# Opening and gate stage of a hybrid backbone step: instruction order written out by hand, row copies on ScalarE, half of the transposes moved behind the modulation

## The chip, the cores and the metric

The kernel runs on one core of a Trainium2 chip. The metric is the device time of one execution in microseconds (us). A change of more than 0.2% (4.4 us) either way counts here as faster or slower.

## The reference, cut to what matters

One layer of a backbone is computed for two groups of tokens, 2048 sample tokens and 128 prompt tokens, each with D = 1024 channels. The part that the change touches is the beginning:

```python
def ada_mod(cvec, w, b):
    m = jnp.einsum('...d,de->...e', jax.nn.silu(cvec), w) + b
    return jnp.split(m, 3, axis=-1)
...
    shift, scale, gate = ada_mod(c, w_ada[l], b_ada[l])
    xn = rmsnorm(h, ln_g[l]) * (1.0 + scale[:, None, :]) + shift[:, None, :]
    # in mixer:
    proj = jnp.einsum('btd,de->bte', xn, w_in)
    # z_a: 512 columns of proj; silu(z_a) gates branch A
```

Everything behind it (the rest of the projection, a delta-rule scan, a spatial gating branch, a Fourier branch, the merge and the output projection) is unchanged.

## The kernel before

**Numbers.** Each f32 operand of a matmul is split into a high and a low f16 part, and three products are summed: high by high, high by low and low by high. `xh` and `xl` hold the two parts of the modulated, normalised input, turned so that channels lie on partitions (8 blocks `k` of 128 channels by 2176 tokens). A weight block is handled by the generator `converting` (from L262): ScalarE squares it and sums, VectorE casts the sum (L234), TensorE sums over the partitions, VectorE makes a power-of-two scale (L243 to L245), ScalarE writes the high part (L290), VectorE the low part (L291). `zlo` and `zhi` are these parts for the four blocks of `z_a`.

**Opening.** The shift and the scale come from 16 blocks of `w_ada`, each 512 KB, loaded into a ring of 7 buffers (`ab`). Six of them (6, 7, 12 to 15) are stored turned: VectorE multiplies such a block with a row of SiLU(cond) and sums (`column_sums`, L490, one instruction for each of the two groups). The other ten go in pairs through TensorE (`block_pair`): eight f32 matmuls give two rows of 256 sums, VectorE copies them out of PSUM (`adr`, L497), and TensorE turns them into columns in the bank `pa` (L499). Between these blocks the first 512 token rows (`x0`, four loads) arrive. TensorE turns them, 8 blocks of 4 transposes (L543), and ScalarE copies each block out (L544). ScalarE also squares the rows (L460), which gives a factor per token. `row_scale` spreads it over partitions by matmuls and copies it to `rsb` (L473). `bound(0)` adds the bias to the shift and `bound(1)` makes the scale, with a bound from which a common power of two `sx` follows; then both are multiplied with it. The loads stand in one list:

```python
LOADS = ("a0", "a1", "d6", "x0", "x1", "x2", "a2", "a3", "x3", "d7", "a4", "a5", "w0", "d12", "a8", "a9", "w1", "d13", "d14", "a10", "d15", "a11")
```

Here `a` is a block for TensorE, `d` one for VectorE, `x` a quarter of the rows, and `w` a weight block of `z_a`. The loads are kept in this order on SyncE's queue. The first two weights are converted inside this stage, the other two in the gate stage.

**Gate stage.** The tokens are taken in five groups `ti`: four of 512 and one of 128 (the prompt). For each group and each `k`, VectorE multiplies `x` with the scale and `rsb` (L612), ScalarE adds the shift and rounds to `xh` (L613), and the low part is the rest. VectorE makes the low part in one instruction (L627), GpSimd in two (L623, L624). GpSimd has `k` = 2 and 5 of the first group and all odd `k` of the others. `silu_za` then runs 24 matmuls of 512 columns for each of four blocks of `z_a`: first blocks 0 and 1 together, then 2, then 3. `finish` takes a block out of PSUM: ScalarE a sigmoid (L601), VectorE the product (L602), SyncE the store. `row_scale` for the next group stands after the first two blocks.

**Order.** The program is traced in the order in which it is written, and a planner then lays out each engine's instruction stream by priority and by simulated readiness. The stream of an engine can thus differ from the order of the text. `tc.issue_after(i)` forces instructions of an engine behind the instruction `i` of the same engine, and costs no wait on another engine. Before, some ten such places hold single instructions back. Waits between engines follow from the data, and each engine works through its stream in order.

Of the kernel before, what the change touches and what calls it, by code (L numbers as in the profile page):

```python
# [11 lines left out]
F16 = mybir.dt.float16  # L12
# [26 lines left out]
LOADS = ("a0", "a1", "d6", "x0", "x1", "x2", "a2", "a3", "x3", "d7", "a4", "a5", "w0", "d12", "a8", "a9", "w1", "d13", "d14", "a10", "d15", "a11")  # L39
# [129 lines left out]

@with_exitstack  # L170
def hybrid_flow_kernel(ctx: ExitStack, tc: tile.TileContext, x_prompt, x_sample, state_delta, c, c_ctx, w_ada,
# [3 lines left out]
    V, A, G, PE, SY = nc.vector, nc.scalar, nc.gpsimd, nc.tensor, nc.sync  # L175
# [237 lines left out]
    warm = sb(cp, [P, 1], "warm")  # L413
    A.activation(warm, mhalf, AF.Sigmoid)
# [36 lines left out]
    def norms(xs, early=False, after=None):  # L451

        xss = sb(p0p, [P, len(xs)], "xss")
        for j, x in enumerate(xs):
            jk = spare(after is not None and j == 3) if early else sb(p0p, [P, D], "xm", F16, bufs=4)
            with tc.issue_after(after[min(j // 2, 1) + j // 3].ins) if after is not None else ExitStack():
                if after is not None and j == 3:
                    V.scalar_tensor_tensor(jk, x, 1.0, x, ALU.mult, ALU.mult, accum_out=xss[:, j:j + 1])
                else:
                    A.activation(jk, x, AF.Square, accum_out=xss[:, j:j + 1])  # L460
        rs = sb(p0p, [P, len(xs)], "rs")
        rsqrt(rs, xss, 1.0 / D, len(xs))
        return rs

    def row_scale(ti, xs, after=None):

        t0, tn = TBS[ti]
        rs = norms(xs, ti < 2, after)
        ps = bank(ps_x, [P, len(xs), P])
        for j in range(len(xs)):  # L470
            mm(ps[:, j, :], rs[:, j:j + 1].to_broadcast([P, P]), ident)
        rsb = sb(p0p, [P, tn], "rsb", bufs=1)
        V.tensor_copy(rsb, ps.rearrange("p j t -> p (j t)"))  # L473
        return rsb

    rowc = [sb(p0p, [P, D], "rowc") for g in range(2)]
    for g in range(2):
        for half in range(2):
            ps = bank(ps_mm, [P, 4, P])
            for k in range(4):  # L480
                mm(ps[:, k, :], scT[:, half * 4 + k, g:g + 1].to_broadcast([P, P]), ident)
            A.copy(rowc[g][:, half * 512:half * 512 + 512], ps.rearrange("p k c -> p (k c)"))
# [3 lines left out]
    raw0 = sb(p0p, [P, KT, 512], "xt")  # L486

    def column_sums(b, st):
        for g in range(2):
            V.scalar_tensor_tensor(spare(1), st, 1.0, rowc[g], ALU.mult, ALU.mult, accum_out=ada[:, b, g:g + 1])  # L490

    def block_pair(b, sts):
        ps = bank(ps_d, [2, 256])
        for k in range(KT):
            mm(ps, scT[:, k, :], sts[k // 4][:, k % 4 * 256:(k % 4 + 1) * 256], k == 0, k == KT - 1)
        adr = sb(p0p, [2, 256], "adr", bufs=1)
        V.tensor_copy(adr, ps)  # L497
        for k in range(2):
            PE.transpose(pa[:, b + k, :], adr[:, k * P:(k + 1) * P], ident[:2, :2])  # L499

# [14 lines left out]
    x0, half = None, None  # L515
    for what in LOADS:
        kind, n_ = what[0], int(what[1:])
        if kind == "w":
            read_next()
            fetch(n_ + 1)  # L520
            while len(wdone) - len(wsteps) <= n_:
                weight_step()
            wlate[0] = 0
            continue
        st = sb(p0p, [P, 4, D], "xt") if what == "x0" else None if kind == "x" else sb(p0p, [P, D], "ab", bufs=7)
        if kind == "x":
            x0 = st if n_ == 0 else x0
            st = x0[:, n_, :]
        load(st, xrows(n_ * P, P) if kind == "x" else w_adb[n_])
        if kind == "d":  # L530
            column_sums(n_, st)
        elif kind == "a" and n_ % 2:
            if n_ == 11:
                bound(0)
            block_pair(n_ - 1, (half, st))
        elif kind == "a":
            half = st
        elif n_ == 3:
            x0 = [x0[:, j, :] for j in range(4)]
            for k in range(KT):  # L540
                ps = bank(ps_mm, [P, 512])
                for j in range(4):
                    PE.transpose(ps[:, j * P:(j + 1) * P], x0[j][:, k * P:(k + 1) * P], ident)  # L543
                A.copy(raw0[:, k, :], ps)  # L544
            rsb = row_scale(0, x0)
# [14 lines left out]
    with tc.high_priority():  # L560
        bound(1)
        bs16 = sb(cp, [P, 1], "bs16", BF16)
        V.tensor_add(bs16, bss[:, 0:1], bss[:, 1:2])
        sx, isx = scales(None, cp, "xsc", bs16)
        V.tensor_scalar(ms, ms, sx, None, ALU.mult)
        V.tensor_scalar(sh, sh, sx, None, ALU.mult)
        for w in wdone:
            V.tensor_mul(w.inv, w.own, isx)
# [5 lines left out]
    def silu_za(ti, gs, between=None):  # L574
# [8 lines left out]
        for i, phase in enumerate(phases):  # L583
            if i == 1 and between is not None:
                between()
# [6 lines left out]
        else:  # L592
            with tc.issue_after(zaw[3].made.ins), tc.issue_after(zaw[3].low.ins):
                finish(ti, gs, pss)
# [1185 lines left out]
```

## Time and profile before

| | |
|---|---|
| time, median of 3 runs | 2192.6 us (2190.14 to 2194.45) |
| profiled execution, its own time | 2190.57 us |
| span of its profile | 2188.8 us |
| TensorE busy | 2110.8 us (96%) |
| VectorE, ScalarE, GpSimd busy | 1314.2, 1034.0, 735.5 us |
| mean granted TensorE clock | 0.988 |

Start times are in us from the span's start. In a row of the timeline stand the start, the duration, the engine and line, the operation, output and input by name, shapes and count; in brackets the idle time before it and what ended that. PE is TensorE, DVE VectorE, ACT ScalarE, POOL GpSimd. A row that merges n matmuls shows a span that is a little longer than n times their pitch, since matmuls overlap. The gate stage's first matmul begins at 43.56 us, and the next stage's first at 151.19 us.

### The profile page before, as it was taken

To read this page: it belongs to the slowest core of one execution; us is meant where nothing else is said; L and a number is where in the kernel's file an instruction comes from. 1 tells how busy PE (TensorE), PEld (TensorE's weight loads), DVE (VectorE), ACT (ScalarE), POOL (GpSimd) and SP (SyncE) were. 2 spreads that over 40 slices of the span, in tenths; PEclk is the share of its full clock that TensorE was granted. 3 is DMA by queue.
4 is the path that set the end of the run, shared out by engine and by line. 5 is a ranking of instruction groups with operands and counts; after the bars stand their busy time and mean duration, and the time that the engine had idled before them with its cause. 6 is when DMAs were issued, how large, how long until landed. Compare 5 with 4: busy or idle time off the path is not lost. (4 is left out here: it accounts for less than half of the span.)

```text
span 2188.8 us, 42552 instructions
## 1 busy us (share of the span) xinstructions
PE 2110.8 (96%) x16249; PEld 1206.4 (55%) x16249; DVE 1314.2 (60%) x3035; ACT 1034.0 (47%) x2372; POOL 735.5 (34%) x889
## 2 busy tenths in 40 slices
PE   7899999999899999999899999899999999999998
PEld 3354444455455577778555555555655444444444
DVE  5646854479878697456665555765564544233454
ACT  4544744466555574445644445655553422222332
POOL 2531332223334332443322223355443222122543
PEclk9999999999999999999999999999999999999999
DMA  8524832177776653434645546766664433323542
GB/s 340 192 95 153 287 118 100 61 221 232 232 230 216 213 170 105 122 115 140 217 163 168 164 160 190 231 200 209 205 199 157 164 125 118 131 101 119 177 149 106
DMA packets 228012, 371.90 MB, mean 170 GB/s; under 512 B 38728, under 2 KB 125152, under 8 KB 225376
## 3 DMA queue, kind: packets, MB, share of 16 engines
q1 hardware_dynamic: 175424, 274.20, 38.6%
q0 software_dynamic: 12688, 51.27, 6.6%
q10 hardware_dynamic: 39696, 43.72, 6.0%
q8 instruction: 127, 2.08, 0.4%
q14 instruction: 77, 0.63, 0.1%
HBM read 241.48 MB, written 127.62 MB: 169 GB/s over the span
## 5 line engine op out<-in xcount | busy, mean ns | idle before, releaser
L220 PE MATMUL b<-xh,whi 128*128 128x512 f16 (+1 forms) x1920 | 651.9, 348 | 7.5 <-DVE sg L1325 5.7
L220 PE MATMUL b<-xl,whi 128*128 128x512 f16 (+1 forms) x1920 | 652.6, 348 | 0.0
L220 PE MATMUL b<-xh,wlo 128*128 128x512 f16 (+1 forms) x1920 | 651.1, 348 | 0.0
L220 PEld LDWEIGHTS <-whi 128*128 128x128 f16 x3904 | 356.5, 98 | 336.7 <-issue 18.5
L220 PEld LDWEIGHTS <-wlo 128*128 128x128 f16 x1952 | 191.5, 98 | 177.6 <-issue 3.8
L220 PE MATMUL b<-big,bhi 128*128 128x512 f16 (+1 forms) x960 | 250.7, 347 | 3.4 <-ACT big L1557 2.5
L1597 POOL TENSOR_TENSOR mrow<-mrow,sg 128x512 f32<-128x512 f32 (+1 forms) x80 | 95.4, 1193 | 284.5 <-DVE sg L1596 175.6
L220 PE MATMUL b<-big,blo 128*128 128x512 f16 (+1 forms) x480 | 162.9, 347 | 0.2 <-DVE blo L291 0.2
L1587 ACT ACTIVATE sg<-b,winv 128x512 f32<-128x512 f32 (+1 forms) x120 | 74.2, 618 | 135.0 <-PE b L220 134.2
L220 PEld LDWEIGHTS <-xh 128*128 128x128 f16 x1496 | 117.0, 98 | 30.3 <-DVE yT L1510 1.9
L1596 DVE SCALAR_TENSOR_TENSOR sg<-b,binv,sg 128x512 f32<-128x512 f32 (+1 forms) x80 | 53.4, 668 | 129.1 <-PE b L220 121.4
L220 PEld LDWEIGHTS <-bhi 128*128 128x128 f16 x960 | 86.4, 98 | 80.2 <-issue 3.6
L827 POOL TENSOR_TENSOR cy<-cy,raw 128x545 f32<-128x545 f32 (+1 forms) x48 | 65.7, 1397 | 186.3 <-ACT raw L826 186.3
L234 DVE CAST wscb<-wss 128x1 bf16<-128x1 f32 x93 | 14.2, 153 | 143.7 <-ACT wlo L278 59.7
L220 PE MATMUL b<-whi,xh 128*128 128x128 f16 x544 | 92.9, 219 | 2.3 <-DVE yT L1510 1.7
L1060 POOL COPY T<-ES 32x256 f16<-32x256 f16 x68 | 27.1, 399 | 198.1 <-DMA ES<-ei 193.2
L220 PE MATMUL b<-whi,xl 128*128 128x128 f16 x544 | 92.9, 219 | 0.0
L220 PE MATMUL b<-wlo,xh 128*128 128x128 f16 x544 | 92.9, 219 | 0.0
L220 PE MATMUL b<-wohi,ml 128*128 128x512 f16 (+2 forms) x248 | 91.7, 372 | 0.5 <-DVE ml L1668 0.5
L220 PE MATMUL b<-wohi,mh 128*128 128x512 f16 (+2 forms) x248 | 91.9, 372 | 0.0
L220 PE MATMUL b<-wolo,mh 128*128 128x512 f16 (+2 forms) x248 | 91.9, 372 | 0.0
L291 DVE SCALAR_TENSOR_TENSOR wlo<-wst,wsc,whi 128x1024 f16<-128x1024 f32 x52 | 69.0, 1327 | 32.6 <-ACT whi L290 32.4
(476 smaller groups left out, 4283.0 us busy)
## 6 DMA issues: line engine op xcount, KB each, us to landing
wst<-in_w_blk_dram SPq DMA_DIRECT2D x58, 512.0 KB, 5.0
qkv<-cy POOLq DMA_DIRECT2D x12, 1089.0 KB, 5.3
st<-br SPq DMA_DIRECT2D x48, 256.0 KB, 3.9
mrow<-mrg SPq DMA_DIRECT2D x18, 512.0 KB, 3.7
mrow<-mrg SPq DMA_DIRECT2D x16, 576.0 KB, 3.9
mrg<-mrow POOLq DMA_DIRECT2D x16, 576.0 KB, 3.7
dc<-dec SPq DMA_DIRECT2D x17, 512.0 KB, 4.7
kq<-qkv SPq DMA_DIRECT2D x34, 256.0 KB, 4.2
```

The lines of the kernel that those rows point to most:

```text
L220: PE.matmul(out, l, r, start=start, stop=stop)
L234: V.tensor_copy(sb16, ss)
L291: w.low = V.scalar_tensor_tensor(w.lo, st, s, w.hi, ALU.mult, ALU.subtract)
L827: G.tensor_tensor(y[:, c0:c1], y[:, c0:c1], raw[:, 1 + c0:1 + c1], ALU.mult)
L1060: G.tensor_copy(T16[rows(a0, b), :, :, b], ES[0:32, :, 2 * a0 + b, :, wT])
L1587: A.activation(sg, ps, AF.Sigmoid, scale=gw.inv)
L1596: V.scalar_tensor_tensor(sg, ps, binv[:, 1:2], sg, ALU.mult, ALU.mult)
L1597: G.tensor_tensor(mr, mr, sg, ALU.add)
```

## The change

Three helpers of the kernel, the handles for VectorE, ScalarE and TensorE, are wrapped. While `kept` is set, each instruction of such an engine is put behind the one written before it on the same engine, so that its stream is the text's order. GpSimd and SyncE are not wrapped. `kept` is set from the opening to the end of the gate stage, but for the conversion of the small weight `w_bd` and for the weight steps of the next stage (`loose_steps`). The text itself is rewritten:

- The loads come as a0 a1 d6, x0 to x3, d7 a2 a3, d12 a4 a5 w0, d13 w1, a8 a9, d14 a10 d15 a11.
- The copies of the pairs' row sums (`row_copy`) and the copy of the first `rsb` go to ScalarE.
- Of the 8 blocks of transposes of `x0`, four stay around the second pair's matmuls, and four come behind the last pair's (`turn_x0`).
- The first multiply of the gate stage comes ahead of the scaling of the shift.
- In the first group VectorE makes all eight low parts. In the others GpSimd makes those of `k` = 5 and 7 only.
- The conversion of the weights 2 and 3 is threaded through the first group. Their scales come in the middle of the products with the low part.
- The factor of the next group's rows is spread after block 2, ahead of block 3, and block 3 is taken out of PSUM behind the fourth multiply of the next group.

```diff
+class _InTurn:
+    def __init__(self, tc, engine):
+        self.tc, self.engine, self.kept, self.last = tc, engine, False, None
+    def __getattr__(self, name):
+        f = getattr(self.engine, name)
+        if not self.kept:
+            return f
+        def call(*args, **kw):
+            with self.tc.issue_after(self.last.ins) if self.last is not None else ExitStack():
+                self.last = f(*args, **kw)
+            return self.last
+        return call
...
-    V, A, G, PE, SY = nc.vector, nc.scalar, nc.gpsimd, nc.tensor, nc.sync
+    G, SY = nc.gpsimd, nc.sync
+    V, A, PE = [_InTurn(tc, e_) for e_ in (nc.vector, nc.scalar, nc.tensor)]
...
+    V.kept = A.kept = PE.kept = True
...
+    def row_copy(ps):
+        adr = sb(p0p, [2, 256], "adr", bufs=1)
+        A.copy(adr, ps)
+        return adr
+    def turn_x0(k):
+        ps = bank(ps_mm, [P, 512])
+        for j in range(4):
+            PE.transpose(ps[:, j * P:(j + 1) * P], x0[:, j, k * P:(k + 1) * P], ident)
+        A.copy(raw0[:, k, :], ps)
...
+    p_ = block_pair(0)
+    column_sums(6, 0)
+    squares(x0s, xss0, (0, 1), True)
+    column_sums(6, 1)
+    adr = row_copy(p_)
+    turn_rows(0, adr)
...
+    rsb = spread(rs, A)
+    column_sums(12, 0)
+    column_sums(12, 1)
+    fetch_blocks(13)
+    read_next()
+    p_ = block_pair(4)
...
+    step0()
+    adr = row_copy(p_)
+    column_sums(13, 0)
+    step0()
+    fetch_blocks(8, 9)
+    turn_rows(4, adr)
+    step0()
+    step1()
+    column_sums(13, 1)
+    step1()
+    step0()
+    fetch_blocks(14, 10, 15, 11)
+    p_ = block_pair(8)
+    step1()
+    step1()
+    adr = row_copy(p_)
+    turn_rows(8, adr)
+    bound(0)
+    column_sums(14, 0)
+    column_sums(14, 1)
+    p_ = block_pair(10)
+    column_sums(15, 0)
+    column_sums(15, 1)
+    adr = row_copy(p_)
+    turn_x0(4)
+    turn_x0(5)
+    turn_rows(10, adr)
+    turn_x0(6)
+    turn_x0(7)
...
+        def low(k):
+            x, hi, lo = part_of(k)
+            if ti and k in (5, 7):
                 G.tensor_scalar(x, x, sh[:, k, g:g + 1], None, ALU.add)
                 G.tensor_tensor(lo, x, hi, ALU.subtract)
             else:
+                V.scalar_tensor_tensor(lo, x, sh[:, k, g:g + 1], hi, ALU.add, ALU.subtract)
+        for k in range(KT):
+            x, hi, _ = part_of(k)
+            V.scalar_tensor_tensor(x, x, ms[:, k, g:g + 1], rsb, ALU.mult, ALU.mult)
...
+            A.activation(hi, x, AF.Identity, bias=sh[:, k, g:g + 1])
...
+            if k == 3 and late is not None:
+                finish(*late)
...
+            for k in range(KT):      # first group
+                if k == 3:
+                    for w in two:
+                        next(w)
+                if k < 6:
+                    low(k)
+            def others():
+                for w in two:
+                    next(w)
+                low(6)
+                low(7)
+                for w in two:
+                    next(w, 0)
...
+            zp = silu_za(ti, (0, 1))
+            if ti < 4:
+                rs = root(xss)
+            finish(*zp)
+            zp = silu_za(ti, (2,))
+            if ti < 4:
+                rsb = spread(rs, V)
+            finish(*zp)
+            if ti > 1:
+                loose_steps()
+            late = silu_za(ti, (3,))
```

More of the change, by code (lines that the diff above doesn't have):

```diff
@@ L449, in row_blocks @@
         return xs
[L451 to L462, printed above, removed]
-        return rs
@@ new lines, in root, with spread @@
+    def root(xss):
+        n_ = xss.shape[-1]
+        rs = sb(p0p, [P, n_], "rs")
+        rsqrt(rs, xss, 1.0 / D, n_)
+        return rs
+    def spread(rs, on):
+        n_ = rs.shape[-1]
+        ps = bank(ps_x, [P, n_, P])
+        for j in range(n_):
+            mm(ps[:, j, :], rs[:, j:j + 1].to_broadcast([P, P]), ident)
+        rsb = sb(p0p, [P, n_ * P], "rsb", bufs=1)
+        ps = ps.rearrange("p j t -> p (j t)")
+        if on is A:
+            A.copy(rsb, ps)
+        else:
+            V.tensor_copy(rsb, ps)
@@ L474, in row_scale, with row_group @@
         return rsb
     rowc = [sb(p0p, [P, D], "rowc") for g in range(2)]
[L477 to L482, printed above, removed]
+    def row_group(i):
+        g, half = i // 2, i % 2
+        ps = bank(ps_mm, [P, 4, P])
+        for k in range(4):
+            mm(ps[:, k, :], scT[:, half * 4 + k, g:g + 1].to_broadcast([P, P]), ident)
+        A.copy(rowc[g][:, half * 512:half * 512 + 512], ps.rearrange("p k c -> p (k c)"))
```

203 lines of the change are left out of this document (97 added, 106 removed).

## The prediction

> **What bounds the kernel now.** I read the page's first line and then TensorE's share by stretch.
>
> ```profile
> span 2188.8 us, 42552 instructions
> ...
> 42.00:77.00 35.00, 26.34 (x109) 11.57 (x109) 18.61 (x42) 16.02 (x28) 12.70 (x5) 0.86 0.73 265
> 77.00:104.00 27.00, 23.99 (x108) 10.93 (x107) 21.88 (x29) 18.94 (x32) 21.11 (x14) 0.94 0.47 176
> 104.00:152.00 48.00, 48.00 (x302) 25.52 (x300) 28.69 (x57) 23.67 (x45) 23.96 (x28) 1.00 0.27 98
> 152.00:2189.00 2037.00, 1981.58 (x15570) 1141.24 (x15568) 1223.05 (x2853) 958.26 (x2240) 676.12 (x836) 0.99 0.51 166
> ...
> 96.00:100.00 4.00, 3.46 (x10) 1.24 (x10) 4.00 (x6) 3.01 (x6) 3.66 (x2) 0.57 0.94 386
> ```
>
> The columns are the stretch, its length, the busy time of PE, PEld, DVE, ACT and POOL, the granted clock, the DMA share and GB/s. From 104 to 152 us TensorE has no gap, and behind 152 us it is idle 55.4 of 2037 us. So what the gate stage finishes earlier, the end gets, unless the later stages change. Up to 104 us TensorE has gaps, and twice a lower clock. The timeline of TensorE shows what ends each gap.
>
> ```profile
> 33.32 1.89 PE L220 MATMUL b<-ab,scT 128*2 128x256 f32 x8 [0.41 <-DMA ab<-in_w_adb_dram]
> 39.76 0.37 PE L499 MATMUL b<-cst,adr 2*128 2x2 f32 x2 [4.55 <-DVE adr L497]
> ...
> 43.56 1.01 PE L220 MATMUL b<-xh,zhi 128*128 128x512 f16 x2 [2.39 <-ACT xh L613]
> ...
> 51.13 1.03 PE L220 MATMUL b<-xl,zhi 128*128 128x512 f16 x4
> 55.54 4.28 PE L220 MATMUL b<-xl,zhi 128*128 128x512 f16 x12 [3.39 <-POOL xl L624]
> ...
> 63.20 1.90 PE L220 MATMUL b<-xh,zhi 128*128 128x512 f16 x8 [1.63 <-ACT zhi L290]
> ...
> 76.74 0.59 PE L220 MATMUL b<-xh,zhi 128*128 128x512 f16 x2 [2.08 <-ACT xh L613]
> ...
> 96.54 0.59 PE L220 MATMUL b<-xh,zhi 128*128 128x512 f16 x1 [2.96 <-DVE sg L602]
> ```
>
> The last blocks of `w_ada` have arrived at 33.3, yet the first gate matmul starts only at 43.56. In the gate stage TensorE waits for GpSimd's low part (3.39), a weight (1.63), the next group's first `xh` (2.08) and a PSUM bank that VectorE empties late (2.96). All are matters of order on VectorE, ScalarE and GpSimd, and these I follow next.
>
> **The opening.**
>
> ```profile
> 8.58 1.23 DVE L490 SCALAR_TENSOR_TENSOR xl<-ab,rowc 128x1024 f16<-128x1024 f32 x1 [4.84 <-DMA ab<-in_w_adb_dram]
> ...
> 39.29 0.41 DVE L497 COPY adr<-b 2x256 f32<-2x256 f32 x1
> 39.63 0.14 DVE L510 TENSOR_TENSOR ms<-ada,pc 128x8 f32<-128x8 f32 x1
> 40.17 0.17 DVE L510 TENSOR_TENSOR ms<-b,pc 128x8 f32<-128x8 f32 x1 [0.39 <-PE b L499]
> ...
> 42.01 5.38 DVE L612 SCALAR_TENSOR_TENSOR xt<-xt,ms,rsb 128x512 f32<-128x512 f32 x8
> ```
>
> ```profile
> L490 DVE SCALAR_TENSOR_TENSOR xl<-ab,rowc 128x1024 f16<-128x1024 f32 x12 | 14.6, 1214 | 7.9 <-DMA ab<-in_w_adb_dram 4.8 <-ACT rowc L482 3.0
> ...
> L544 ACT COPY xt<-b 128x512 f32<-128x512 f32 x8 | 4.3, 593 | 4.2 <-PE b L543 2.4 <-PE b L220 1.8
> ...
> L291 DVE SCALAR_TENSOR_TENSOR zlo<-wst,wsc,zhi 128x1024 f16<-128x1024 f32 x2 | 2.6, 1282 | 1.2 <-ACT zhi L290 1.2
> ...
> L497 DVE COPY adr<-b 2x256 f32<-2x256 f32 x5 | 2.0, 410 | 2.0 <-PE b L220 1.8
> ```
>
> VectorE sets the start: the last pair's rows lie in PSUM at 35.2, but their copy comes at 39.29, behind the column sums. Loads land at an even pace: the third at 8.58 (VectorE's wait for block 6 ends there), the 22nd and last of the list at 33.3 (TensorE's wait), so 1.30 us each. By the new list d13 is the 15th and lands at 24.2, d15 the 21st at 32.0. From d13 on VectorE has six column sums (1.21, with the read of the sum about 1.25: 7.5 us), two low parts of weights (1.28 each: 2.6), `bound(0)`, two casts and six scale steps at 0.14 to 0.17 each (about 1.3), and it waits for ScalarE's high parts about 1.7 us, since the second weight's scale stands behind `block_pair(8)` on TensorE and its low part ahead of the sums of 14 and 15. That ends at 24.2 + 7.5 + 2.6 + 1.3 + 1.7 = 37.3. The five copies of 0.41 us are off it. They cost nothing on ScalarE, whose idle time before its 42.79 row (below) is 8.31 us; the four late copies of `x0` (0.59 each) and the last row copy end near 37.3 under the same cover. Were it gone, about 0.6 us would be paid. The last rows are in `pa` by then (33.3, matmuls to about 34.4, copy, transposes: 35.5), so nothing waits for them.
>
> Behind it stand `bound(1)` and the scale of `sx`: from 39.63 to 42.01, less the wait of 0.39 and 0.25 for the scaling of the shift and of two weights, which move behind the first multiply: 1.8. The first multiply starts at 39.2. From there to the first matmul it was 1.55 (42.01 to 43.56), now 0.15 more, since the shift's scaling stands between. So 40.8 in place of 43.56: **-2.8 us**. Its bounds: not before 38.0 (d15 at 32.0 and two sums, 34.5), not after 43.4 if VectorE still ends its sums at 39.3.
>
> **The first group.**
>
> ```profile
> 42.79 5.36 ACT L613 ACTIVATE xh<-xt,sh 128x512 f16<-128x512 f32 x8 [8.31 <-DVE xt L612]
> ...
> 62.00 2.19 ACT L290 ACTIVATE zhi<-ab,wsc 128x1024 f16<-128x1024 f32 x2 [9.55 <-DVE wsc L244]
> ```
>
> ```profile
> 47.31 4.06 DVE L627 SCALAR_TENSOR_TENSOR xl<-xt,sh,xh 128x512 f16<-128x512 f32 x6
> ...
> 61.62 0.22 DVE L243 TENSOR_SCALAR wsc<-b 128x1 int32<-128x1 int32 x2 [10.12 <-PE b L220]
> ...
> 63.18 2.48 DVE L291 SCALAR_TENSOR_TENSOR zlo<-ab,wsc,zhi 128x1024 f16<-128x1024 f32 x2 [0.84 <-ACT zhi L290]
> ```
>
> ```profile
> 44.95 9.42 POOL L623 TENSOR_SCALAR xt<-xt,sh 128x512 f32<-128x512 f32 x2 [26.25 <-ACT xh L613]
> 54.34 2.26 POOL L624 TENSOR_TENSOR xl<-xt,xh 128x512 f16<-128x512 f32 x2
> ```
>
> ```profile
> L278 ACT ACTIVATE zlo<-ab 128x1024 f16<-128x1024 f32 x2 | 2.1, 1039 | 0.0
> ```
>
> The high products take 7.57 us (43.56 to 51.13, part of it below the full clock; TensorE is as idle ahead of it in the new order, so I keep that): 40.8 to 48.4. VectorE multiplies until about 44.8, makes low parts at 0.68 each (4.06 by 6), waits for ScalarE's second square of a weight (1.04 each, behind the last `xh`) until about 47.8 and has six low parts at 50.0. TensorE then has four of eight low blocks done (8 matmuls took 1.90 at 63.20 with their overlap, so 0.22 a matmul, and two for each block), reaches the scale matmuls at 50.1, VectorE needs 0.8 us for the scales, and the low parts 6 and 7 are there at 51.8 and 52.5: TensorE waits about 1.1 us in all and ends with blocks 0 and 1 at 54.8. The high parts of weights 2 and 3 start at 51, not 62.0, so block 2 starts at 54.8. Before, from first matmul to block 2 it was 63.20 - 43.56 = 19.6, now 14.0: **-5.6 us**. From 54.8 block 2 (24 matmuls, 5.2 us), the spread and block 3 follow; the next `rsb` is made at 61, `xh` at 64, needed at 66: the 2.08 us go (**-2.1**). The next x lands long before: its loads wait for buffers that free until 37.5, and 4 MB take about 11 us at the pace above.
>
> **The later groups.**
>
> ```profile
> L601 ACT ACTIVATE sg<-b,winv 128x512 f32<-128x512 f32 x16 | 10.4, 678 | 21.3 <-PE b L220 21.3
> L602 DVE SCALAR_TENSOR_TENSOR sg<-b,winv,sg 128x512 f32<-128x512 f32 x16 | 11.7, 743 | 11.4 <-ACT sg L601 11.3
> L612 DVE SCALAR_TENSOR_TENSOR xt<-xt,ms,rsb 128x128 f32<-128x128 f32 x8 | 2.2, 348 | 0.1
> L612 DVE SCALAR_TENSOR_TENSOR xt<-xt,ms,rsb 128x512 f32<-128x512 f32 x32 | 24.1, 819 | 0.1
> L623 POOL TENSOR_SCALAR xt<-xt,sh 128x128 f32<-128x128 f32 x4 | 2.7, 684 | 3.5 <-ACT xh L613 3.5
> L624 POOL TENSOR_TENSOR xl<-xt,xh 128x128 f16<-128x128 f32 x4 | 1.7, 441 | 0.2
> L624 POOL TENSOR_TENSOR xl<-xt,xh 128x512 f16<-128x512 f32 x14 | 17.4, 1252 | 0.0
> L627 DVE SCALAR_TENSOR_TENSOR xl<-xt,sh,xh 128x512 f16<-128x512 f32 x18 | 16.5, 966 | 0.0
> ...
> 77.69 4.12 POOL L623 TENSOR_SCALAR xt<-xt,sh 128x512 f32<-128x512 f32 x2 [8.29 <-ACT xh L613]
> ```
>
> The bank wait of 2.96 goes, since `finish` of the late block now stands behind the fourth multiply, and with it the half clock behind it (4 us at 0.57: 1.7): **-4.6**. What is late next? Call T the end of a group's block 3. VectorE has four multiplies done, then sigmoid and product of block 3 (0.68, 0.74) until T + 1.6, so the fifth `xh` is there at T + 3.1; TensorE comes to it after 16 matmuls, T + 3.5. It just fits. GpSimd gets `k` = 5 at T + 3.7 and runs two scalings (2.06 each, its pace in the second group) and two subtractions (1.25): the last low part at T + 10.4, needed at T + 9.9. VectorE's low parts, at 0.97 beside GpSimd, cost up to as much. I take 1.0 us for each of three groups: **+3.0**, between 0 and the case of a starved GpSimd below.
>
> [...]
>
> The prompt group has only 2.6 us of matmuls for blocks 0 and 1 (48, a quarter as long), but behind T the chain of sigmoid, product, four short multiplies (4 x 0.35) and two pairs on GpSimd (2 x 1.13) is 5.1 us. In before this group was mixed with the last blocks of the group ahead; now the order forbids it. I take **+2.0**; at best 0, if the planner puts matmuls of the next stage in between, which are not pinned, at worst 2.5 and 1.7 for a half clock.
>
> **The sum.** -2.8 - 5.6 - 2.1 - 4.6 + 3.0 + 2.0 = -10.1 us. The profiled execution took 2190.57 (1.8 beyond its span): 2180.5. The median of the runs is 2.0 above it: **2182.6 us**.
>
> **The rivals.** *GpSimd starves* (slower). In the first group GpSimd's two scalings took 9.42 us while VectorE ran without a gap, and its low parts ended at 56.6, 5.2 us behind VectorE's. In the new order VectorE's stream in each group is as dense. If that happens in the groups 1 to 3, VectorE ends at T + 10, GpSimd at T + 15.3, needed at T + 9.9: 5.4 us and a half clock behind it (1.7), three times: 21 us in place of my 3. Then 2182.6 + 18 = 2200.6. It beats the gain from 4.4 us a group. For it: the 9.42 row; against it: the 4.12 row, where VectorE multiplied all the time. [...]
>
> *The opening does not shorten, and the strict order waits in more places.* If VectorE ends its sums at 39.3 as before and the fifth `xh` comes 1 us late in each group, 5.5 us of the gain are gone: about 2188.
>
> *The later stages give it back.* Their order is planned from simulated times, and these now start otherwise. If the 55.4 us of gaps behind 152 us grew by a fifth, 11 us, nothing would be left: about 2193, either way by 4.
>
> *The order was that already.* If the planner's streams were nearly those of the text, only the five copies (2.0 us) count: 2190.6. Against it: VectorE's four waits above, which the new text orders otherwise.
>
> **How the numbers follow.** Forecast 0.65, with a range of its own from 2176 (no new stall) to 2188; the second rival 0.12, GpSimd 0.11, the later stages 0.09, the same order 0.03. By over 0.2% (4.4 us, about what a measurement of this kernel can tell) faster: 0.65 + 0.08 of the second rival + 0.02 of the third = 0.75. Within it: 0.04 + 0.04 + 0.03 = 0.11. Slower: 0.11 + 0.03 = 0.14. The range 2174 to 2192 leaves out the starved GpSimd, half of the later stages' case and the best end, about 0.19.
>
> **What would show it.** Right: the first `xh` matmul near 40.8, block 2 near 55, no wait for L602 near the second group's block 3, the next stage's first matmul near 141 in place of 151. Wrong: L624 as TensorE's releaser with over 2 us a group; a column sum of block 15 that ends after 39; or the gate stage over at 141 and the gaps behind it grown.

## The result, and the profile after

The changed kernel takes 2189.27 us (median of 12 runs, 2183.73 to 2191.87), the kernel before in the same comparison 2192.04. The ratio is 0.9984, with a 95% interval of 0.9975 to 0.9993: 0.16% faster, inside the 0.2% that counts as a difference. Forecast were 2182.6 us (the terms of its sum give 2182.5) and a range of 2174 to 2192. The profiled execution took 2189.06 us.

The first line of the changed kernel's profile, and its busy time by the same stretches as before:

```profile
span 2186.8 us, 42541 instructions
...
42.00:77.00 35.00, 32.47 (x148) 14.70 (x148) 29.28 (x57) 25.61 (x43) 6.81 (x5) 0.95 0.77 280
77.00:104.00 27.00, 25.78 (x121) 12.01 (x121) 18.23 (x24) 13.49 (x22) 10.17 (x7) 1.00 0.48 163
104.00:152.00 48.00, 46.01 (x430) 26.60 (x427) 27.88 (x62) 23.75 (x42) 10.97 (x15) 1.00 0.29 99
152.00:2187.00 2035.00, 1973.56 (x15388) 1137.40 (x15388) 1217.64 (x2846) 954.86 (x2237) 674.29 (x833) 0.99 0.52 166
```

From 42 to 104 us TensorE has 7.9 us more work done than before, and no half clock behind the first group (a granted clock of 1.00 from 77 to 104 us, 0.94 before). But it now has gaps between 104 and 152 us (2.0 us), and behind 152 us it is idle for 61.4 us in place of 55.4.

The timeline of TensorE in the changed kernel. All instructions made through the wrapped handles carry the wrapper's line, L182; L239 is the helper of the matmuls behind the gate stage.

```profile
32.95 3.61 PE L182 MATMUL b<-ab,scT 128*2 128x256 f32 x16
...
42.58 1.01 PE L182 MATMUL b<-xh,zhi 128*128 128x512 f16 x2 [2.39 <-ACT xh L182]
53.28 1.26 PE L182 MATMUL b<-xl,zhi 128*128 128x512 f16 x4 [1.06 <-DVE xl L182]
56.10 1.89 PE L182 MATMUL b<-xh,zhi 128*128 128x512 f16 x8
...
67.38 0.59 PE L182 MATMUL b<-xh,zhi 128*128 128x512 f16 x2
...
76.99 1.02 PE L182 MATMUL b<-xl,zhi 128*128 128x512 f16 x4 [0.82 <-DVE xl L182]
78.55 1.02 PE L182 MATMUL b<-xl,zhi 128*128 128x512 f16 x4 [0.54 <-DVE xl L182]
100.16 1.14 PE L182 MATMUL b<-xl,zhi 128*128 128x512 f16 x4 [0.26 <-POOL xl L696]
101.72 0.59 PE L182 MATMUL b<-xl,zhi 128*128 128x512 f16 x2 [0.42 <-POOL xl L696]
...
152.66 0.21 PE L239 MATMUL b<-bdp,xh 128*128 128x32 f16 x1 [1.75 <-issue]
...
898.81 0.18 PE L239 MATMUL b<-ES,N 128*128 128x32 f16 x1 [4.96 <-POOL T L1167]
```

Block 2 of the first group starts at 56.10 (before 63.20), the second group at 67.38 without a wait (before 76.74), and the waits for a bank (2.96) and for GpSimd (3.39) are gone. At 100 us the gate stage is some 12 us ahead. Two rows at the end are new: a gap of 1.75 us amid short matmuls at 152.66, and one of 4.96 us at 898.81.

To see where the 12 us go I paired each matmul with the same one of the kernel before (same operands and shape, same place in their sequence) and subtracted the start times. This *lead* of one profiled execution each, a median over the matmuls around the time given (in the row's own kernel), is the frame for all that follows. At 115 us the order of matmuls in e3, f4, g1 and h2 differs from that of the kernel before, and their leads there are good to about 1.5 us only. The last column is the ratio to the kernel before from the timed runs.

| kernel | lead at 115 | 200 | 850 | 900 | 2100 us | median us | ratio, 95% interval |
|---|---|---|---|---|---|---|---|
| changed | 11.4 | 6.1 | 4.1 | 0.0 | 1.9 | 2189.27 | 0.9984 [0.9975, 0.9993] |
| e0, the same again | 11.3 | 7.5 | 6.8 | 2.3 | 0.2 | 2186.83 | 0.9975 [0.9966, 0.9984] |
| e1, level's matmul back | 9.8 | 5.9 | 4.8 | 0.9 | 1.1 | 2188.18 | 0.9988 [0.9978, 0.9997] |
| e2, q/k/v held | 11.2 | 1.3 | 1.1 | 2.3 | 3.6 | 2187.18 | 0.9985 [0.9973, 0.9996] |
| e3, no order kept | 10.8 | 10.6 | 10.5 | 13.2 | 16.1 | 2178.57 | 0.9941 [0.9927, 0.9954] |
| f1, state behind sums | 10.6 | 6.3 | 5.1 | 7.6 | 5.4 | 2179.40 | 0.9942 [0.9925, 0.9958] |
| f2, free from group 2 | 5.6 | 3.6 | 5.8 | 6.9 | 8.3 | 2183.24 | 0.9959 [0.9943, 0.9975] |
| f3, opening kept only | 7.5 | 7.3 | 0.5 | 0.4 | 0.2 | 2187.32 | 0.9979 [0.9969, 0.9989] |
| f4, e3 with copies on VectorE | 12.6 | 12.6 | 6.2 | 6.4 | 3.2 | 2187.38 | 0.9974 [0.9963, 0.9985] |
| g1, f4, VectorE's place held | 13.0 | 13.0 | 6.1 | 8.8 | 4.5 | 2186.08 | 0.9972 [0.9963, 0.9981] |
| g2, f1, two sums earlier | 11.0 | 6.9 | 6.8 | 7.9 | 7.9 | 2180.50 | 0.9952 [0.9937, 0.9966] |
| g3, small parts alone | -1.3 | -1.3 | -3.6 | -1.9 | -5.3 | 2194.27 | 1.0009 [0.9998, 1.0021] |
| g4, GpSimd four low parts | 8.3 | 0.8 | -6.1 | -3.6 | -8.4 | 2194.61 | 1.0015 [1.0002, 1.0027] |
| h1, f1, long before short | 11.0 | 8.2 | 7.0 | 9.2 | 9.1 | 2180.41 | 0.9940 [0.9926, 0.9953] |
| h2, f4, ScalarE's place held | 11.2 | 11.2 | 11.0 | 15.0 | 8.4 | 2183.04 | 0.9958 [0.9946, 0.9971] |

Executions of one kernel lie up to 5.5 us from their median (the 12 runs above), so a lead at the end can be that far from the median: f1's profiled execution took 2185.61, above its median of 2179.40, and e3's 2174.73, below its median. Leads at one place are safer, since the rows around them show the wait that made the step.

### The profile page after: what moved, and what is told of

Read it like the earlier page. It is cut to its first block, busy times and chain, and to the rows that moved or that the text cites. A ratio compares the mean times of both kernels' runs of the same rounds, so it can differ in the third digit from the quotient of the medians.

```text
span 2186.8 us, 42541 instructions
## 1 busy us (share of the span) xinstructions
PE 2108.4 (96%) x16249; PEld 1208.5 (55%) x16249; DVE 1314.1 (60%) x3039; ACT 1037.0 (47%) x2378; POOL 704.8 (32%) x869
## 5 line engine op out<-in xcount | busy, mean ns | idle before, releaser
L239 PE MATMUL b<-xh,whi 128*128 128x512 f16 (+1 forms) x1920 | 650.9, 348 | 8.7 <-DVE sg L1432 6.0
L239 PE MATMUL b<-xl,whi 128*128 128x512 f16 (+1 forms) x1920 | 651.6, 348 | 0.0
L239 PE MATMUL b<-xh,wlo 128*128 128x512 f16 (+1 forms) x1920 | 650.7, 348 | 0.0
L239 PEld LDWEIGHTS <-whi 128*128 128x128 f16 x3904 | 356.3, 98 | 335.7 <-issue 16.6
L239 PEld LDWEIGHTS <-wlo 128*128 128x128 f16 x1952 | 191.3, 98 | 177.1 <-issue 2.8
L239 PE MATMUL b<-big,bhi 128*128 128x512 f16 (+1 forms) x960 | 250.7, 347 | 4.5 <-ACT big L1664 3.1
L239 PE MATMUL b<-big,blo 128*128 128x512 f16 (+1 forms) x480 | 162.9, 347 | 0.2 <-DVE blo L310 0.2
L239 PEld LDWEIGHTS <-xh 128*128 128x128 f16 x1496 | 118.3, 99 | 28.9 <-issue 1.8
L239 PEld LDWEIGHTS <-bhi 128*128 128x128 f16 x960 | 86.4, 98 | 80.9 <-issue 4.2
L239 PE MATMUL b<-wlo,xh 128*128 128x128 f16 x544 | 94.6, 221 | 0.0
L239 PE MATMUL b<-whi,xh 128*128 128x128 f16 x544 | 94.6, 221 | 0.0
L239 PE MATMUL b<-whi,xl 128*128 128x128 f16 x544 | 94.5, 221 | 0.0
L253 DVE CAST wscb<-wss 128x1 bf16<-128x1 f32 x89 | 13.6, 153 | 133.7 <-ACT wlo L297 55.4
L239 PE MATMUL b<-wohi,mh 128*128 128x512 f16 (+2 forms) x248 | 91.9, 372 | 0.0
L239 PE MATMUL b<-wolo,mh 128*128 128x512 f16 (+2 forms) x248 | 91.9, 372 | 0.0
L239 PE MATMUL b<-wohi,ml 128*128 128x512 f16 (+2 forms) x248 | 91.7, 372 | 0.0
```

What stands on the lines that cost most here:

```text
L239: PE.matmul(out, l, r, start=start, stop=stop)
L253: V.tensor_copy(sb16, ss)
```

## The experiments

**First round: is it the planner's two moves?** Behind the gate stage the two kernels' TensorE order differs mainly in two places. The planner pulled the first 24 matmuls of the q/k/v projection into the gate stage, so the decays' 272 short ones follow the prompt group directly; and the first matmul of the scan's first level (`ES`, `N`) stands ahead of a block of the projection, where it waits 4.96 us.

e0 is the changed kernel once more.

> The changed kernel once more, beside the next three on one chip. Both theories: about 2189 us, 0.998 of before, with the gate stage 11 to 12 us ahead of before when the prompt group's first matmul begins, about 6 us ahead at 200 us, and about 2 us ahead at the end.

e1 puts the level's matmul back:

```diff
+                with tc.issue_after(newest[0].ins) if (d, t, h, a) == (0, 16, 0, 0) else ExitStack():
                     mm(ps[:, h, a], Nf[:, ...], ES[:, h, 2 * a + b0, 0, wT])
```

> The changed kernel with one matmul put back: the first matmul of the scan's first level (N by ES, 32 columns) goes behind the projection block ahead of it, as before, where the planner had put it in front. Theory 1 (the later loss comes from re-planned order): TensorE's wait of 5.0 us near 899 us falls to about 1.7, so 3.3 us less than the changed kernel, about 2186. Theory 2 (whatever the gate stage saves is lost to chains in the scan that run at their own pace): the wait moves to another place and the time stays at about 2189.

e2 holds the first column's projection behind the gate stage:

```diff
+                with tc.issue_after(PE.last.ins) if ct == 0 else ExitStack():
                     gemm_T(ps, w, 0, xh[:, :, t0:t0 + tn], xl[:, :, t0:t0 + tn])
```

> The changed kernel with the first q/k/v column's matmuls held behind the last matmul of the gate stage, so that 120 long matmuls no longer fill in among the gate's and 24 of them stand again between the prompt group and the 272 short matmuls of the decays. Theory 1: the gap of 1.7 us inside the short matmuls and the half clock of 6.8 us (3.4 us lost) go, about 5 us; the planner also puts the scan's first-level matmul back by itself (3.3 us). Together about 2181. Theory 2: about 2189, the gain ahead of 200 us shows and is gone by 900 us. [...]

e3 has the new text and the copies, but the wrapper keeps no order (only the conversion of `w_bd` and the loose weight steps are still held behind what stands ahead of them):

```diff
-            with self.tc.issue_after(self.last.ins) if self.last is not None else ExitStack():
+            with ExitStack():
                 self.last = f(*args, **kw)
```

> The changed kernel with its text, copies and transposes, but with the pinning off: the planner lays out VectorE, ScalarE and TensorE. Theory A (the pinned order is what shortens the gate stage): the waits on the way to the second group come back in part, the second group starts near 72 instead of 68 us, and the time is about 2193. Theory B (the new text, the division of the low parts and the copies do it): the gate stage is as early as pinned, and the time about 2189.

e0 measured the same as the changed kernel, 2186.83. e1 brought nothing (2188.18): TensorE still loses the lead at 900 us, since with `ES` behind the block it waits there for the sums `yT`:

```profile
897.52 0.29 PE L241 MATMUL b<-whi,xh 128*128 128x128 f16 x1 [4.31 <-DVE yT L1620]
```

So the `ES` row alone was not the cause: in these two executions its wait ended at 898.81 and the other at 897.52, and taking away one leaves the other. e2 brought nothing at the end either (2187.18), but its timeline shows what the 24 matmuls had covered:

```profile
124.23 1.02 PE L182 MATMUL b<-xl,zhi 128*128 128x512 f16 x4 [1.74 <-DVE xl L182]
125.79 1.02 PE L182 MATMUL b<-xl,zhi 128*128 128x512 f16 x4 [0.54 <-DVE rs L182]
140.54 0.27 PE L182 MATMUL b<-xh,zhi 128*128 128x128 f16 x2 [2.20 <-ACT xh L182]
143.71 0.37 PE L182 MATMUL b<-xl,zhi 128*128 128x128 f16 x2 [1.14 <-DVE xl L182]
145.42 0.80 PE L182 MATMUL b<-xl,zhi 128*128 128x128 f16 x6 [1.34 <-POOL xl L696]
```

These are 7.0 us of waits in the last groups, and a lower clock with them (0.68 from 140 to 145 us, 0.64 from 145 to 150); the lead falls from 11.2 us to 1.3. In the changed kernel 24 long matmuls of 0.22 us, 5.2 us of work, lie in those places. The surprise was e3: without any kept order the new text takes 2178.57 us, 12 us less than the kernel before, and keeps its lead to the end.

**Second round: where in the order.** What stops TensorE at 900 us is read from VectorE's timeline. First the changed kernel:

```profile
891.49 0.69 DVE L1211 SCALAR_TENSOR_TENSOR v<-sv,v 128x512 f16<-128x512 f32 x1 [3.85 <-ACT v L1210]
894.87 0.48 DVE L1327 TENSOR_SCALAR S<-S,usc 128x512 f32<-128x512 f32 x1 [2.68 <-DMA S<-in_state_delta_dram]
896.05 0.69 DVE L1211 SCALAR_TENSOR_TENSOR S<-S,S 128x512 f16<-128x512 f32 x1 [0.70 <-ACT S L1210]
896.66 0.59 DVE L1616 TENSOR_TENSOR yT<-b,us 128x256 f32<-128x256 f32 x1
897.09 0.59 DVE L1617 TENSOR_TENSOR yT<-b,us 128x256 f32<-128x256 f32 x1
```

The scaling of the scan's first state `S` waits for the state's load, and behind it in the queue stand the last two sums for `yT`, which the block of the projection on TensorE needs. In the kernel before, and in e2 and e3, the sums stand ahead of the scaling; in the changed kernel and e1 behind it. f1 puts this one instruction back:

```diff
-                V.tensor_tensor(yv[:, 64 - k0:64 - k1:-1, :], uc[:, n0:8, :], us[:, n0:8, :], ALU.subtract)
+                sums.append(V.tensor_tensor(yv[:, 64 - k0:64 - k1:-1, :], uc[:, n0:8, :], us[:, n0:8, :], ALU.subtract))
...
+                    with tc.issue_after(sums[-1].ins) if d == 0 else ExitStack():
                         V.tensor_scalar(S2, S2, us, FS, ALU.mult, ALU.mult)
```

> The changed kernel with one further order: the scaling of the recurrence's first state on VectorE may only follow the last pair of sums that makes yT (in the changed kernel it stands ahead of that pair and waits for the state's load until 894.87, and TensorE then waits 4.96 us at 898.8; in the kernel before it stands behind the pair). Theory 'given back in the later stages': at that place the wait falls to about 2 us, and with the half clock behind it the end comes 3 to 4 us sooner than the changed kernel's: about 2183 to 2185 us. Rival 'the later stages take up whatever is won' (what is won at 900 is lost again by 1100, as the first level's matmul put back on its own was): no difference at the end, 2187 to 2189.

VectorE, and behind it TensorE, in f1:

```profile
891.95 0.60 DVE L1619 TENSOR_TENSOR yT<-b,us 128x256 f32<-128x256 f32 x1
892.39 0.59 DVE L1620 TENSOR_TENSOR yT<-b,us 128x256 f32<-128x256 f32 x1
892.87 1.15 DVE L1330 TENSOR_SCALAR S<-S,usc 128x512 f32<-128x512 f32 x1
```

```profile
893.04 0.23 PE L241 MATMUL b<-whi,xh 128*128 128x128 f16 x1 [0.24 <-DVE yT L1620]
```

The wait of 4.96 us is 0.24. The lead rises from 6.1 to 7.6 us at this place, where the changed kernel's falls from 5.1 to 0.0: 3.3 us by the longer wait (4.96 for 1.71), the rest behind it, where the granted clock was 0.73 from 900 to 905 us (in f1 1.00 from 892 to 901). It rises because the kernel before waits there itself:

```profile
900.65 0.23 PE L220 MATMUL b<-whi,xh 128*128 128x128 f16 x1 [1.71 <-DVE yT L1510]
```

The time is 2179.40, 7 to 9 us under the changed kernel's by the ratios (0.9942 against 0.9975 and 0.9984): twice what I expected, and near what the two steps of the lead add up to, 1.5 and 5.1. This one place is shown to be the largest part of the missed gain. The scaling is not shown to be enough by itself: in f1 the planner also put the `ES` matmul behind the block again (902.4 us), and the two left together.

f2 and f3 keep the order in a part only (the wrapper's flag is set as shown, and `last` is still noted):

```diff
     for ti, (t0, tn) in enumerate(TBS):
+        V.kept = A.kept = PE.kept = ti < 2      # f2; ti < 0 in f3
```

> The changed kernel, with the written order kept only in the opening and the groups 0 and 1, and VectorE, ScalarE and TensorE free to be planned from group 2 on. Theory 'the written order costs at the gate stage's end' (VectorE's and ScalarE's order in groups 2, 3 and the prompt group leaves TensorE some 5 to 7 us of waits, which early q/k/v matmuls cover only in part): the lead over the kernel before is about 10 us at 165 us instead of 6 to 7.5, there is no gap behind the first 160 short matmuls of the decays, and the end comes at 2178 to 2181 us. Rival 'it is the opening's and the first groups' order that costs': the lead stays 6 to 7.5 us at 165 us, the end near 2187 to 2189.

> The changed kernel, with the written order kept in the opening alone, up to the scale of sx; free from group 0 on. Theory 'the written order costs at the gate stage's end, and gains in the first group': the second group starts 1 to 2 us later than in the changed kernel, the lead at 165 us is 9 to 10 us, the end at 2179 to 2182 us. Rival 'the new text and the copies gain, no order kept does': the lead at 165 us is 10.6 as without any kept order, the end at 2177 to 2179 us.

Both my theory and its rival missed here. With the order given up from group 2 on, f2's lead at 200 us is 3.6, not 10: the wait for a bank that VectorE empties late is back.

```profile
112.64 0.38 PE L182 MATMUL b<-xh,zhi 128*128 128x512 f16 x1 [3.73 <-DVE sg L182]
```

The same wait is there in f3 (3.30) and f4 (2.30), and not in the changed kernel. So the kept order does prevent it, as forecast, though e3, which keeps none, is free of it too; and it is not simply the last groups' order that costs. f3, with the opening alone kept, has its first gate matmul at 44.61 and 7.3 us at 200. Only without any kept order do the planner's choices reach 10.6 to 12.6. Which single pin costs what, I cannot say; that stays open. f3 then loses nearly 8 us at a place that f4 reaches at 827 us and shows better.

f4 is e3 with the five row copies and the first `rsb` copy on VectorE again:

```diff
-        A.copy(adr, ps)
+        V.tensor_copy(adr, ps)
...
-    rsb = spread(rs, A)
+    rsb = spread(rs, V)
```

> The new text with no order kept, and the five row copies and the copy of the first rsb back on VectorE. Theory 'these copies lie off the path': at most 1 us later than with them on ScalarE, 2178 to 2180 us. Rival 'the copies are what gains': most of the 12 us goes, 2186 to 2190 us.

The lead at 200 us is 12.6, larger than with the copies on ScalarE (10.6), so the copies are not what gains. But the end is 2187.38: the lead is lost at 827 us. TensorE's row and, from the same execution, ScalarE's queue (ACTq is its issuing of DMAs):

```profile
827.44 0.29 PE L239 MATMUL b<-whi,xh 128*128 128x128 f16 x1 [4.55 <-DVE yT L1617]
```

```profile
820.26 3.97 ACTq L979 DMA_DIRECT2D n<-n  x1
824.34 0.63 ACT L1063 ACTIVATE n<-n 128x512 f16<-128x512 f32 x1 [5.38 <-issue]
...
825.95 0.37 ACT L1612 COPY us<-b 128x256 f32<-128x256 f32 x1 [0.98 <-DVE n L1064]
```

**Third round: the second place, and the parts by themselves.** g1 holds in f4, on VectorE, the low part of the last product of the scan's preparation behind the fourth pair of sums, and the state's scaling as in f1:

```diff
+            with tc.issue_after(sums[3].ins) if (t, d) == (15, 1) else ExitStack():
                 V.scalar_tensor_tensor(p16[:, 1, :], q_, 1.0 / FS, p16[:, 0, :], ALU.mult, ALU.subtract)
```

> The new text with no order kept and the copies on VectorE, as in the last run, with two orders held in the later stages: on VectorE the low part of the last normalised product may only follow the fourth pair of sums of yT (as it does in the kernel before; without it VectorE waited 4.6 us for ScalarE ahead of that pair, and TensorE 4.55 us at 827), and the scaling of the first state only the last pair. Theory 'the later stages' new order takes the gain': the lead of 12.6 us at 165 us stays to the end: 2176 to 2180 us, 7 to 11 us sooner than without the two orders. Rival 'what is won there is lost at the next place': 2185 to 2188 us.

The rival came: 2186.08, and the lead still falls from 13.0 to 6.1. VectorE's instruction was not the cause; the sums wait for the copy `us` on ScalarE, which in f4 stands behind a DMA issue of 3.97 us and others. h2 (fourth round) holds ScalarE's high parts of that chunk behind the copy, in f4 with the state's scaling as in f1:

```diff
+            with tc.issue_after(rows4[3].ins) if t == 15 else ExitStack():
                 made = A.activation(p16[:, 0, :], q_, AF.Copy, scale=1.0 / FS)
```

> The new text with no order kept and the copies on VectorE, the scaling of the first state behind the last sums, and on ScalarE both high parts of the last chunk's products behind the copy of the fourth block of rows (in the kernel without this that copy came at 825.95, behind four DMA issues of 0.5 to 4.0 us and those high parts, and TensorE waited 4.55 us for the sums that need it). Theory 'the copy's place on ScalarE is the cause at 827': the wait there falls under 2 us, the lead of 12.6 us at 165 us is still 10 us or more at 1000, and the end comes at 2178 to 2182 us. Rival 'TensorE only arrives sooner at a chain that others set': the wait stays 3 us or more, or comes back at the next step, and the end at 2185 to 2188 us.

The wait at 827 is gone and the lead is 15.0 us at 900. Then 5.9 us of it go at one new wait and the lower clock behind it (0.58 from 902 to 906 us), as the list of TensorE's waits in h2 has it:

```profile
PE b L241 <- DMA N<-n: 4.4, 1, 4.4
```

The end, 2183.04, lies 4 us below f4's and 3 below g1's, in intervals that overlap, and between theory and rival. By the trace the cause of the wait at 827 is shown, and so is that the next place can take back a part.

g2 takes f1 and moves two column sums of the opening into VectorE's waits:

```diff
     column_sums(13, 0)
+    column_sums(13, 1)
     step0()
...
     step1()
+    column_sums(14, 0)
     step1()
```

> The changed kernel with the state's scaling behind the last sums, and two column sums moved in the opening: the second sum of block 13 ahead of the first weight's scale, the first sum of block 14 ahead of the second weight's low part, where VectorE waited 2.03 us for TensorE and 1.16 us for ScalarE. Theory 'VectorE's own waits are what the opening lost': its sums end about 2.3 us sooner (36.5 to 37), the first gate matmul comes at 40.0 to 40.6 in place of 42.6, and the end 1 to 2 us sooner than with the state's order alone: 2177 to 2179 us. Rival 'the loads or TensorE set it': the sums end at 38 to 39, and nothing moves.

VectorE's sums end at 37.9 in place of 39.1 in the changed kernel, and yet the first gate matmul comes at 43.03. VectorE now waits for TensorE's last pair, which took 5.30 us in place of 3.61, as the clock from 34 to 38 us was granted at 0.57 in this execution (1.00 in the changed kernel's):

```profile
39.61 0.17 DVE L182 TENSOR_TENSOR ms<-b,pc 128x8 f32<-128x8 f32 x1 [1.52 <-PE b L182]
```

The outcome is the rival's: two chains of nearly the same length lead to the scale, and shortening one uncovers the other. e0 and h1, with the changed kernel's opening, had the dip as well (5.30 us for the last pair), and their first gate matmul came at 42.76 and 43.04, so in such an execution the moved sums gain nothing. Without the dip about 1 us might remain; that is not shown.

g3 is the kernel before with the small parts alone (the copies on ScalarE; four of the eight blocks of transposes written behind the loads), the two later places held as before:

```diff
-        V.tensor_copy(adr, ps)
+        A.copy(adr, ps)
...
-            for k in range(KT):
+            for k in range(4):
+                turn_x0(k)
...
+    for k in range(4, KT):
+        turn_x0(k)
     read_next(p0p)
```

> The kernel before with the two small parts alone: the five row copies and the copy of the first rsb on ScalarE, and the transposes of the blocks 4 to 7 of the first x written behind the loads; the rest of its text stays, no order kept, and the two orders of the later stages held as the kernel before has them. Theory 'the parts are off the path': a lead of 0 to 1 us at 165 us, the end at 2190 to 2192 us. Rival 'VectorE's 2.0 us of copies count in full': the first gate matmul 2 us sooner, 2188 to 2189 us.

The ratio is 1.0009 [0.9998, 1.0021]: by themselves the parts bring nothing at the end. At the start they do, in the one profiled execution: the first gate matmul comes at 42.65, 0.9 us sooner than before and about as early as in the changed kernel (42.58), so the gain of 1.0 in the opening is not shown to come from the kept order. The gate stage loses it again (TensorE waits 4.05 us for GpSimd's low part, 3.39 before, and the granted clock from 77 to 104 us is 0.88 for 0.94), and 2.6 us more go at the place of 827, where the copy `us` stands behind a DMA issue of 3.70 us again.

g4 gives GpSimd all four odd blocks again, in the changed kernel with the two later places held:

```diff
-            if ti and k in (5, 7):
+            if ti and k % 2:
```

> The changed kernel with GpSimd making the low parts of all four odd blocks in the groups 1 to 3 and the prompt group, as in the kernel before, in place of two; the two orders of the later stages held. Theory 'GpSimd's two pairs just fit': four pairs take about 13.5 us from T + 3.7 and are needed by T + 9.9, so TensorE waits for GpSimd 5 to 7 us in each of three groups, the next stage starts 15 to 20 us later than in the changed kernel, and the end comes at 2193 to 2200 us. Rival 'GpSimd has room': TensorE waits under 2 us a group, the end at 2178 to 2183 us.

The time is as expected (2194.61), the way is not. GpSimd is not late: TensorE waits for it 0.34 and 0.52 us in the groups 1 and 2, and 0.75 in the prompt group. VectorE is. Its multiplies from 60 to 150 us, by lines, in f1 and in g4:

```profile
L182 DVE SCALAR_TENSOR_TENSOR xt<-xt,ms,rsb 128x512 f32<-128x512 f32 x24 | 16.4, 744 | 0.0
```

```profile
L182 DVE SCALAR_TENSOR_TENSOR xt<-xt,ms,rsb 128x512 f32<-128x512 f32 x24 | 23.1, 1022 | 0.0
```

They take 1022 ns in place of 744, so `xh` comes late (4.4 us of waits in six places, 0.4 in f1), and the lead at 200 us is 0.8, 5.5 less than in f1. Another 6 us are lost far behind the low parts, at the place of 827: TensorE waits 4.78 us for `yT` at 840.50, and the copy `us` stands behind a DMA issue of 3.86 us. So the time that I expected came partly by luck. By the rows GpSimd's share changes VectorE's times more than GpSimd's own: the multiplies took 1022 ns in g4 and 744 in f1, the low parts 828 ns in g4 and 1123 in f1, while GpSimd's two instructions took 1998 and 1377 ns in g4 and 2060 and 1577 in f1. Why the instructions take longer is not shown.

**Fourth round: the short matmuls.** h1 takes f1 and puts 24 long matmuls of the second tile ahead of the 272 short ones; the first 24 stay in the gate stage.

```diff
-    pace.start(decays(), 1.2)
...
                 gemm_T(ps, w, 0, xh[:, :, t0:t0 + tn], xl[:, :, t0:t0 + tn])
+                if (ct, t0) == (0, 512):
+                    pace.start(decays(), 1.2)
...
+                    with tc.issue_after(long.ins) if k == 0 else ExitStack():
                         mm(pb[:, t - c0, :], xh[:, k, ts], bdp[:, k, :], k == 0, k == KT - 1)
```

> The changed kernel with the state's scaling behind the last sums, and the 272 short matmuls of the decays behind the second 24 long matmuls of the first q/k/v column (the first 24 go into the gate stage as before, where they fill waits). Theory 'the borrowed matmuls are paid back at the short ones': with 24 long matmuls ahead of them the short ones run without the gap of 0.9 to 1.7 us and at the full clock, as in the kernel before; the lead at 165 to 200 us is 8.5 to 9.5 us in place of 6.3 to 6.9, the end 2 to 3 us sooner than with the state's order alone: 2176 to 2178 us. Rival 'the short ones cost that wherever they stand in this kernel': gap and half clock stay, the lead is 6 to 7 us, 2179 to 2181 us.

The stretches of the short matmuls, in the changed kernel and in h1:

```profile
150.00:155.00 5.00, 3.25 (x124) 3.15 (x121) 0.30 (x1) 1.77 (x3) 0.00 (x0) 0.68 0.69 219
155.00:160.00 5.00, 5.00 (x46) 2.36 (x43) 1.71 (x8) 4.06 (x7) 0.00 (x0) 0.64 0.01 3
```

```profile
150.00:155.00 5.00, 5.00 (x116) 3.66 (x115) 0.16 (x1) 2.00 (x4) 0.00 (x0) 1.00 0.71 229
155.00:160.00 5.00, 5.00 (x179) 4.60 (x176) 0.59 (x2) 0.99 (x4) 0.00 (x0) 1.00 0.02 3
```

Gap and half clock are gone (a granted clock of 1.00 in both stretches, 0.68 and 0.64 in the changed kernel), at the same DMA share (0.69 and 0.71). The lead behind the short matmuls is 8.2 us (9.2 up to some 210 us) in place of 6.3, about as expected, and 9.2 at 900. The borrowed matmuls were thus paid back at the short ones. In the medians it does not show (2180.41 and 2179.40, with intervals that overlap), so its worth at the end is open.

e3, f1 and h1 beat the kernel before by about 12 us and the changed one by 7 to 9, and can't be told apart.

## Why the prediction was wrong, point by point

- **Opening, forecast -2.8, measured -1.0** (42.58 for 40.8). The step that failed is VectorE's waits, put at 1.7 us and for the second weight alone. That part measured 1.88: 0.73 for the scale behind `block_pair(8)` and 1.15 for the high part. The first weight's scale stands behind `block_pair(4)` in the same way, and its wait of 2.02 had no term. A pair is eight matmuls in the text and 16 in the trace, and takes 3.61 us (the row at 32.95); the row of 8 at 33.32 (1.89) is the second half of one. So VectorE waited 3.9 us in all, and its sums ended at 39.07, not 37.3, just past the mark that I had named for wrong. The rest held: 39.07 and the forecast's 1.8 and 1.7 behind it give 42.57. VectorE's rows with these waits:

```profile
27.25 0.16 DVE L182 TENSOR_SCALAR wsc<-b 128x1 int32<-128x1 int32 x1 [2.02 <-PE b L182]
...
30.91 0.16 DVE L182 TENSOR_SCALAR wsc<-b 128x1 int32<-128x1 int32 x1 [0.73 <-PE b L182]
...
32.47 1.28 DVE L182 SCALAR_TENSOR_TENSOR zlo<-wst,wsc,zhi 128x1024 f16<-128x1024 f32 x1 [1.15 <-ACT zhi L182]
...
38.99 0.08 DVE L182 DVE_READ_ACCUMULATOR xl<-ab,rowc 128x1 f32 x1
```

- **First group, forecast -5.6, measured -6.1**: block 2 comes 13.5 us after the first matmul (forecast 14.0), with one wait of 1.06 as worked out.
- **Wait before the second group (-2.1) and the bank wait with its half clock (-4.6)**: both gone, as forecast (the granted clock is 1.00 from 77 to 104 us). In f2, where the order is given up from group 2 on, the bank wait returns with 3.73.
- **GpSimd's low parts, forecast +3.0, and the prompt group, +2.0**: 2.0 us of waits are seen in the groups 1 and 2, most of them for VectorE. GpSimd did not starve. For group 3 and the prompt the term was too small: e2 shows 7.0 us and a clock of 0.64 from 145 to 150 us. I had named matmuls of the next stage as what could fill the prompt group; the planner put 24 of them there, and the trace of the changed kernel shows little of it.
- **The stage's end**: the last matmul of the prompt group ends at 146.9 with 5.2 us of borrowed work before it, so the stage's own work is over at 141.7; forecast was 141, for 151 before. The sum held, though not each term.
- **"What the gate stage finishes earlier, the end gets, unless the later stages change."** This step failed, and it decided the result. The lead of 9.6 us at the first short matmul (156.37 before, 146.76 now; 10.1 forecast) is 6.1 behind the short matmuls, since the borrowed work left them without long ones ahead (h1), and 0.0 at 900 us, since the planner put one scaling that waits for a load ahead of two sums, with the `ES` matmul ahead of the block (f1, e1). This is my third rival, "the later stages give it back", with a chance of 0.09. Its price, 11 us, was of the right size: idle time behind 152 us grew by 6.0 us, and the half clock (0.50) of 6.83 us at the short matmuls is worth 3.4 more. The last sign that I had named for wrong, the stage over at 141 and the gaps behind it grown, is what came. The chance was too low: the order behind the gate stage is planned from simulated times, each version got another one, and among the versions of the table that one place or the place at 827 took 5 to 8 us of the lead in six (the changed kernel with its repeat e0, e1, f3, f4, g1, g4).

## What to carry to other kernels

Where a planner lays out the order, a gain at the front is not a gain at the end: pair the same instructions of the two traces, follow the lead to where it steps, and look there for a ready instruction queued behind one that waits on the same engine. Holding one instruction in the place it had may then be worth more than the whole change (f1: 7 to 9 us, with what the planner moved along with it). And an order kept by hand must leave filler for the last groups; what it borrows from the next stage is missing there.

## What the runs showed of the hardware that I had not expected

- The granted clock fell to half for 6.83 us from a gap of 1.75 us amid short matmuls of 32 and 16 columns, as this stretch of the changed kernel shows (the clock is the last but two):

```profile
151.78:158.61 6.83, 5.95 (x120) 4.02 (x120) 1.48 (x7) 3.26 (x7) 0.00 (x0) 0.50 0.33 108
```

  In the kernel before, the clock was 0.57 from 96 to 100 us, behind a wait of 2.96 us.
- The 272 short matmuls stop for 0.9 to 1.7 us behind the 160th of them in five executions in which they follow the prompt group's short matmuls (the changed kernel, e0, e1, f1, g2), and by 0.2 us at most behind 24 long ones (h1 and the kernel before have no gap, f2 the 0.2). In g4 they follow the prompt group too and do not stop; there the prompt group itself had waited 3.2 us, and the granted clock was 0.83 from 145 to 165 us (0.91 in f1). The profile names nothing that the engine waited for; why is not shown.
- Issuing a DMA from ScalarE held its queue for up to 3.97 us (f4), long enough to stop TensorE two engines further on (the wait of 4.55 us at 827.44).
